# A two-layer trunk's attention layer, reordered by hand: 64 query-block steps, and the output projection interleaved with the last head

## Chip, cores and metric

The kernel runs on one core of one Trainium2 chip. The metric is the device time of one execution in microseconds (us). The engines are named as the profile names them: PE (matmul), PEld (weight load), DVE (VectorE), ACT (ScalarE), POOL (GpSimd) and SP, whose queue issues every DMA of this kernel.

## What is computed

The trunk has two layers on x of 1024 tokens by 1024 channels, each `x <- x + Mixer(RMSNorm(x))`, and a final RMSNorm. Layer 0 is a gated short convolution. Layer 1 is causal differential attention with 8 heads of two 64-wide maps each. Cut to what matters here:

```python
proj = h @ w_in                                    # h = rmsnorm(x); 1024 -> 4 * 1024
q, k, v, z = jnp.split(proj, 4, axis=-1)
logits = q_blk . k * 64**-0.5 + bias; causal       # 16 maps, query blocks of 128
p = softmax(logits)
a = p[map 0] - lam * p[map 1]                      # one pair of maps per head
o = rmsnorm(a @ v) * subln_g * (1 - lambda_init)   # per head, 128 wide
x = x + (o * silu(z)) @ w_out
return rmsnorm(x, final_g)
```

## The kernel before

All tensors lie transposed, channels on the partitions. Each weight and activation is split into a rounded part and a remainder ("h" and "l"), so one product is three matmuls per 128-channel slice (`mm3`, L132). A weight unit is a 128x1024 tile: a load (`wr`), an ACT copy that rounds it (`wh`, L119) and a POOL subtraction (`wl`, L120).

**Layer 0** (up to L380) is the same in both kernels but for the ring that its `x2` tiles use. Its last matmuls are the output projection `big<-yh,...`. Then `input_norm` sums the squares (`cps`, L157), takes the power -1/2 on POOL and spreads the row factors into `r_bc`.

**Layer 1** has for each head h: key, query and gate projections (`proj_qk`, `proj_z`: one unit, two halves of 512 tokens, 24 matmuls of 512 columns each), a value projection per pair of heads (`proj_v`, 256 columns a matmul), and 8 query blocks. A block's `scores` are matmuls into a PSUM tile `sc` (L514), a bias addition and a negated maximum on DVE (L517, L519), an exponential on ACT (L521), the combination of both maps on DVE (L528), a split into two f16 parts (ACT L533/L534/L537, POOL L535 or DVE L538), and a DMA that transposes them (L540). `values` multiplies the transposed parts of two blocks with v (L554, tile `av`). `head_norm` squares half a head's output on ACT (L565), splits it into three bf16 parts on POOL (L147, L148), sums columns on PE, takes the power on POOL (L571), writes 512 factors to DRAM (`rrd`), reads them back spread over all partitions (`rb`) and multiplies them in on POOL (L580). `proj_z` then multiplies by the gate on POOL (L407) and stores to `yd`.

The second layer's keys and low parts, `kt` and `qt`, each pass through a DMA that moves 64 partitions (`lo`, L432/L433; `qt`, L439/L440).

**What sets the order.** Python emits heads one after another; `attention(h)` is emitted at a raised priority (`AHEAD = 4000`), and a list scheduler of the language layer, which estimates times, chooses each engine's order from all emitted instructions. Each engine then runs its own queue strictly in that order. `behind` keeps two pairs of blocks between scores and values:

```python
for i, g in enumerate(order(h)):
    for qi in range(2):
        scores(h, g, qi)
        if qi == 0 and len(behind) == 2:
            with tc.issue_after(heads[h]["last", 2 * g].ins):
                attend(*behind.pop(0))
    behind.append((h, i, g))
```

Buffers that matter: PSUM has 3 `mm` tiles, 2 `sc` tiles and 1 `av` tile; `wh`/`wl` have two buffers each, so the unit after next waits for a unit's last matmul.

**The end.** `out_part` computes the output projection for tokens 0 to 511 (8 units of 24 matmuls of 512 columns), then 512 to 767 and 768 to 1023 (16 times 24 matmuls of 256 columns); `finish` applies the final norm and stores.

Of the kernel before, what the change touches and what calls it, by code (L numbers as in the profile page):

```python
# [11 lines left out]
F32 = mybir.dt.float32  # L12
# [10 lines left out]
P = 128  # L23
D = 1024
# [26 lines left out]
def trunk(ctx: ExitStack, tc: tile.TileContext, a: dict, out: bass.AP):  # L51
# [139 lines left out]
    def norm_rows(rsrc, dst, n, tags):  # L191

        for b0 in range(0, n, 4):
            nb = min(4, n - b0)
            dgs = sl.tile([P, 2, nb, P], F32R, tag=tags[b0 // 4 % len(tags)], name="dg")
            dgs = dgs[:, 0], dgs[:, 1]
            spread(rsrc[:, b0:b0 + nb], dgs, V)
            bps = rows(dgs, nb, (psm, "mm") if b0 else None)
# [159 lines left out]
    xh, xl = new_x()  # L358
    acc = sl.tile([P, S], F32, tag=t_acc, name="acc")
    for d in range(KC):  # L360
# [5 lines left out]
        x2 = r_t.tile([P, S], F32, name="x2")  # L366
# [12 lines left out]
    def input_norm():  # L379
        norm_cols([acc, sq], KC, rcol, (r_xr.tile([P, S], F32, name="r1"), r_xr.tile([P, S], BF16, name="r2")))  # L380
        norm_rows(rcol, r_bc, KC, [t_acc, t_xr[0]])


    r_wr.tags.append("wr1")
    heads = [dict() for _ in range(NH)]

    def proj(src, halves=(0, 1)):

        wh, wl = unit(src)
        for half in halves:  # L390
            s = HALF[half]
            pt = psm.tile([P, 512], F32, tag="mm", name="mm")
            mm3(pt, wh, wl, xh, xl, ((0, s.start, 512),))
            yield half, s, pt

    def proj_z(h, keep=None):

        for half, s, pt in proj(a["w_in1"][2 * NH + h]):
            with tc.high_priority():
                zr = sm.tile([P, 512], F32, tag="tq", name="zr")  # L400
                V.tensor_tensor(out=zr, in0=pt, in1=r_bc[:, s], op=ALU.mult)
            th = sm.tile([P, 512], F32, tag="hi", bufs=2, name="th") if keep is None else keep[:, s]
            A.activation(out=th, in_=zr, func=AF.Tanh, scale=0.5)
            V.scalar_tensor_tensor(out=th, in0=th, scalar=1.0, in1=zr, op0=ALU.add, op1=ALU.mult)
            if keep is None:
                o = heads[h]["o"]
                G.tensor_tensor(out=o[:, s], in0=o[:, s], in1=th, op=ALU.mult)  # L407
                dma(out=yd[h, half], in_=o[:, s])

    def proj_qk(h, kind, norm=None):  # L410


        own = (slice(0, HD), slice(HD, P))
        heads[h][kind] = tiles = {}
        if kind == "k":
            for m in range(2):
                tiles[m] = r_k.tile([P, S], F32R, name="kt")
        for half, s, pt in proj(a["w_in1"][(NH if kind == "k" else 0) + h], dict.fromkeys(g // 2 for g in order(h))):
            if norm and half == 0:
                norm()  # L420
            if kind == "q":
                for m in range(2):
                    tiles[m, half] = r_q.tile([P, 2, 512], F32R, name="qt")
            with tc.high_priority():
                tq = sm.tile([P, 512], F32, tag="tq", name="tq")
                if kind == "k":
                    V.scalar_tensor_tensor(out=tq, in0=pt, scalar=HD ** -0.5, in1=r_bc[:, s],
                                           op0=ALU.mult, op1=ALU.mult)
                    lo = sm.tile([P, 512], F32R, tag="lo", bufs=2, name="lo")
                    for m in range(2):  # L430
                        A.activation(out=tiles[m][own[m], s], in_=tq[own[m]], func=AF.Copy)
                        (G, V)[m].tensor_tensor(out=lo[own[m]], in0=tq[own[m]], in1=f(tiles[m])[own[m], s], op=ALU.subtract)  # L432
                        dma(out=f(tiles[m])[own[1 - m], s], in_=f(lo)[own[m]])  # L433
                else:
                    V.tensor_tensor(out=tq, in0=pt, in1=r_bc[:, s], op=ALU.mult)
                    for m in range(2):
                        qt = tiles[m, half]
                        A.activation(out=qt[own[m], 0, :], in_=tq[own[m]], func=AF.Copy)
                        G.tensor_tensor(out=qt[own[m], 1, :], in0=tq[own[m]], in1=f(qt)[own[m], 0, :], op=ALU.subtract)  # L439
                        dma(out=f(qt)[own[1 - m], ::-1, :], in_=f(qt)[own[m]])  # L440

    def proj_v(j, halves=range(4)):


        ws = [unit(a["w_v"][j, i]) for i in range(2)]
        if 0 in halves:
            vh, vl = (r_v.tile([P, KC, 256], F16, name="vt") for part in range(2))
            aux = sm.tile([P, 2, 256], F32, tag="dgl", name="aux")
            sq = sm.tile([P, 256], F32R, tag="sqw", name="sq")
            for k in range(KC):  # L450
                A.activation(out=aux[:, min(k, 1), :], in_=f(ws[k // 4][0])[:, (k % 4) * 256:(k % 4 + 1) * 256],
                             func=AF.Square, scale=g_sb[:, 1, k:k + 1])
                if k:
                    V.tensor_tensor(out=sq if k == KC - 1 else aux[:, 0, :], in0=aux[:, 0, :], in1=aux[:, 1, :], op=ALU.add)
            nps = psa.tile([P, 512], F32, tag="av", name="nps")
            T.matmul(nps[:, :256], lhsT=ones_r, rhs=sq, start=True, stop=True)
            srow = sm.tile([P, 256], F32, tag="srow", name="srow")
            half = aux[:, 1, :].bitcast(I32)
# [3 lines left out]
            sd = aux[:, 0, :].rearrange("p (a b) -> p a b", b=P)  # L462
            G.tensor_tensor(out=sd, in0=srow.rearrange("p (a b) -> p a b", b=P),
                            in1=ident.unsqueeze(1).to_broadcast([P, 2, P]), op=ALU.mult)
            us = sm.tile([P, 2], F32, tag="us", bufs=2, name="us")
            V.reduce_sum(out=us, in_=sd, axis=AX)
            V.reciprocal(out=us, in_=us)
            for h in (2 * j, 2 * j + 1):
                heads[h]["v"] = vh, vl, us[:, h % 2:h % 2 + 1], srow
        vh, vl, _, srow = heads[2 * j]["v"]  # L470
        for tp in halves:
            pt = psm.tile([P, 2, 256], F32, tag="mm", name="mm")
            for i in range(2):
                ts = slice((2 * tp + i) * P, (2 * tp + i + 1) * P)
                for k in range(KC):
                    wh, wl = ws[k // 4]
                    kk = slice((k % 4) * 256, (k % 4 + 1) * 256)
                    T.matmul(pt[:, i, :], lhsT=xh[k][:, ts], rhs=wh[:, kk], start=(k == 0), stop=False)  # L478
                    T.matmul(pt[:, i, :], lhsT=xh[k][:, ts], rhs=wl[:, kk], start=False, stop=False)  # L479
# [292 lines left out]
```

## Time and profile before

| | us |
|---|---|
| median of 3 runs | 1168.45 (1165.59 to 1169.64) |
| the profiled execution's own time | 1168.5 |
| its span, first to last instruction | 1166.7 |
| PE, PEld busy | 1060.6 (91%), 893.4 (77%) |
| DVE, ACT, POOL busy | 605.6 (52%), 425.4 (36%), 573.3 (49%) |
| mean granted TensorE clock | 0.952 of 2.4 GHz |

The span and the execution's time differ by 1.8 us, which lie around the first and last instruction. PE's busy time overlaps between neighbouring matmuls, whose ends are modelled; a busy PE may still run at half clock, which the granted clock tells. "Idle" of an engine that has nothing due costs nothing: what counts is which wait ends last.

### The profile page before, as it was taken

Reading aid. Unit: us, or ns where it says so; the run is one execution under the profiler, and the core shown is the slowest. Engines: PE = TensorE matmul, PEld = TensorE weight load, DVE = VectorE, ACT = ScalarE, POOL = GpSimd, SP = SyncE. Lnnn points to the kernel's source line nnn. Section 1 sums busy time; section 2 is a strip of 40 time slices with the busy share of each in tenths; the row PEclk is TensorE's granted clock in tenths of the full one; section 3 lists DMA queues with packets and bytes.
Section 4 is the critical chain, followed back from the end, with each engine's and each line's share of the span. In section 5 each row is a group of like instructions: output and inputs, shape, how many; then the busy total and the mean of one; then the engine's idle time right before and its main releaser. Section 6 shows DMA issues by size and latency. Waiting matters only on the chain.

```text
span 1166.7 us, 15388 instructions
## 1 busy us (share of the span) xinstructions
PE 1060.6 (91%) x5960; PEld 893.4 (77%) x5960; DVE 605.6 (52%) x945; ACT 425.4 (36%) x705; POOL 573.3 (49%) x355
## 2 busy tenths in 40 slices
PE   8899999999999997999887979979899788984996
PEld 6678888888888885897776869768697677863896
DVE  5573323313314323397676757768588574874123
ACT  3221111111111322366543555536456344463232
POOL 7544334334334442438545575455756556353353
PEclk9899999999999998899899889999899899996998
DMA  5221111111112433335564583644934546475132
GB/s 181 76 71 55 40 51 54 45 47 54 52 40 78 149 123 107 86 71 108 136 101 104 100 143 102 103 110 94 149 88 96 138 82 143 107 177 130 55 113 96
DMA packets 124826, 112.41 MB, mean 96 GB/s; under 512 B 89249, under 2 KB 97105, under 8 KB 124753
## 3 DMA queue, kind: packets, MB, share of 16 engines
q1 hardware_dynamic: 124752, 111.42, 39.4%
q8 instruction: 47, 0.77, 0.3%
q14 instruction: 27, 0.21, 0.1%
HBM read 67.82 MB, written 12.12 MB: 69 GB/s over the span
## 4 chain that ended last, share of the span: by engine, by line
PE 60%; DMA 12%; POOL 10%; issue 8%; DVE 5%; ACT 3%; SPq 1%; POOLq 0%; DVEq 0%; ACTq 0%
PE big L132 35%; PE mm L132 14%; PE sc L514 4%; DMA qt<-qt 3%; DMA rrd<-rr 3%; POOL wl L120 3%; PE av L554 2%; PE mm L479 2%; DMA wr<-in_w_out 2%; PE mm L480 2%; PE mm L478 2%; POOL qt L439 1%; DMA rb<-rrd 1%; DMA p<-p 1%; POOL p L535 1%
## 5 line engine op out<-in xcount | busy, mean ns | idle before, releaser
L120 POOL TENSOR_TENSOR wl<-wr,wh 128x1024 fp32r<-128x1024 f32 x75 | 184.9, 2468 | 257.4 <-ACT wh L119 252.8
L119 ACT ACTIVATE wh<-wr 128x1024 fp32r<-128x1024 f32 x75 | 79.2, 1057 | 314.6 <-PE big L132 293.5
L132 PE MATMUL mm<-xh,wh 128*128 128x512 f32 (+1 forms) x432 | 170.3, 395 | 5.6 <-ACT xh L643 2.5
L132 PE MATMUL mm<-xl,wh 128*128 128x512 f32 (+1 forms) x432 | 170.2, 394 | 4.9 <-POOL xl L644 3.4
L132 PE MATMUL mm<-xh,wl 128*128 128x512 f32 (+1 forms) x432 | 168.8, 394 | 0.9 <-POOL wl L120 0.9
L132 PE MATMUL big<-xh,wh 128*128 128x512 f32 x464 | 143.8, 391 | 2.2 <-DVE cr L289 2.2
L132 PE MATMUL big<-xh,wl 128*128 128x512 f32 x464 | 143.6, 390 | 0.0
L132 PE MATMUL big<-xl,wh 128*128 128x512 f32 x464 | 143.6, 391 | 0.0
L521 ACT ACTIVATE p<-sc,nm 128x256 f32<-128x256 f32 (+7 forms) x128 | 93.8, 736 | 96.4 <-DVE nm L519 55.5
L514 PE MATMUL sc<-kt,qt 128*128 128x512 f32 (+2 forms) x384 | 93.1, 366 | 23.3 <-DMA qt<-qt 21.5
L132 PEld LDWEIGHTS big<-xh,wh 128*128 128x128 f32 x464 | 87.3, 188 | 20.6 <-issue 2.6
L132 PEld LDWEIGHTS big<-xh,wl 128*128 128x128 f32 x464 | 87.6, 189 | 18.2
L132 PEld LDWEIGHTS big<-xl,wh 128*128 128x128 f32 x464 | 87.5, 189 | 18.1
L132 PEld LDWEIGHTS mm<-xl,wh 128*128 128x128 f32 x432 | 83.7, 194 | 21.6 <-POOL xl L644 4.1
L132 PEld LDWEIGHTS mm<-xh,wh 128*128 128x128 f32 x432 | 83.6, 194 | 21.0 <-ACT xh L643 3.1
L132 PEld LDWEIGHTS mm<-xh,wl 128*128 128x128 f32 x432 | 83.8, 194 | 16.5 <-POOL wl L120 1.4
L514 PEld LDWEIGHTS sc<-kt,qt 128*128 128x128 f32 x384 | 68.7, 200 | 34.4 <-issue 23.3
L519 DVE TENSOR_REDUCE nm<-sc 128x2 f32<-128x256 f32 (+5 forms) x96 | 90.9, 950 | 1.3
L554 PE MATMUL av<-p,vt 128*128 128x128 f16 x864 | 59.2, 229 | 24.8 <-DMA p<-p 24.3
L580 POOL TENSOR_TENSOR o<-o,rb 128x512 f32<-128x512 f32 x16 | 20.6, 1286 | 123.5 <-DMA rb<-rrd 114.9
L554 PEld LDWEIGHTS <-vt 128*128 128x128 f16 x864 | 53.0, 103 | 30.5 <-issue 18.2
L479 PE MATMUL mm<-wl,xh 128*128 128x256 f32 x256 | 74.8, 293 | 1.5 <-POOL wl L120 1.5
(174 smaller groups left out, 2026.2 us busy)
## 6 DMA issues: line engine op xcount, KB each, us to landing
wr<-in_w_in SPq DMA_DIRECT2D x53, 512.0 KB, 3.6
wr<-in_w_out SPq DMA_DIRECT2D x16, 512.0 KB, 4.4
qt<-qt SPq DMA_DIRECT2D x32, 256.0 KB, 5.1
xr<-in_xT SPq DMA_DIRECT2D x15, 512.0 KB, 4.4
wr<-in_w_v SPq DMA_DIRECT2D x14, 512.0 KB, 3.7
x2d<-x SPq DMA_DIRECT2D x8, 512.0 KB, 2.9
kt<-lo SPq DMA_DIRECT2D x32, 128.0 KB, 2.7
rb<-rrd SPq DMA_DIRECT2D x16, 256.0 KB, 4.9
```

Source lines behind the costliest of these rows:

```text
L119: A.activation(out=wh, in_=wr, func=AF.Copy)
L120: G.tensor_tensor(out=wl, in0=wr, in1=f(wh), op=ALU.subtract)
L132: T.matmul(ps[:, o:o + n], lhsT=w[:, s], rhs=r[k][:, t:t + n], start=(k == 0 and r is rh and w is wh), stop=(k == KC - 1 and w is wl))
L439: G.tensor_tensor(out=qt[own[m], 1, :], in0=tq[own[m]], in1=f(qt)[own[m], 0, :], op=ALU.subtract)
L478: T.matmul(pt[:, i, :], lhsT=xh[k][:, ts], rhs=wh[:, kk], start=(k == 0), stop=False)
L479: T.matmul(pt[:, i, :], lhsT=xh[k][:, ts], rhs=wl[:, kk], start=False, stop=False)
L480: T.matmul(pt[:, i, :], lhsT=xl[k][:, ts], rhs=wh[:, kk], start=False, stop=(k == KC - 1))
L514: hd["last", qb] = T.matmul(sc[:, i, c0:c1_], lhsT=qt[:, var, ts], rhs=kt[:, c0:c1_], start=(var == 0), stop=(var == 1))
L519: V.tensor_reduce(out=nm[:, ms], in_=sc[:, :, :L], axis=AX, op=ALU.max, negate=True)
L521: A.activation(out=(p1_, p2_)[m][:, :L], in_=sc[:, i, :L], func=AF.Exp, bias=nm[:, m:m + 1], accum_out=st[:, m:m + 1])
L554: T.matmul(av[:, qi * P:(qi + 1) * P], lhsT=v[:, kb, es], rhs=at[:, r, :], start=(kb == 0 and r == 0 and v is vh), stop=(kb == qb and v is ...
L580: G.tensor_tensor(out=o, in0=o, in1=rb, op=ALU.mult)
```

## The change

Layer 1 is put under a manual schedule: every engine runs in the order in which Python emits. The emission is a pipeline of 64 steps, one per query block of each head, step s = 8h + block. A table (`plan`) gives most steps one half projection of a later or earlier head, and the step function writes down the order:

```diff
+    for h in range(1, NH):
+        s0 = 8 * h + 2
+        if h < L7:
+            add_v((h + 1) // 2, (h + 1) % 2, (s0, s0 + 1))
+            add("k", h + 1, (s0 + 2, s0 + 4))
+            add("q", h + 1, (s0 + 3, s0 + 5))
+            add("z", h - 1, (s0 + 6, s0 + 7))
+        else:
+            add("z", L7, (s0, s0 + 1))
+            add("z", h - 1, (s0 + 2, s0 + 3))
...
+    def step(s, score=True):
+        h, qb = divmod(s, 8)
+        for u in loads.get(s, ()):
+            u.load()
+        todo, evict[:] = evict[:], []
+        for fn in todo:
+            fn()
...
+        if last:
+            last.first()
...
+        if score:
+            scores(h, qb)
+        if bounds:
+            half.sums(int(half is last))
+        for u in preps.get(s, ()) if s else ():
+            u.prep()
+        if isinstance(last, Values) and last is not half:
+            last.second()
+        if half and s:
+            half.mm()
+        if last and not isinstance(last, Values):
+            last.second()
+        if 0 <= s - 1 < NS - 1:
+            differences(*divmod(s - 1, 8))
+        if last:
+            last.third()
+        store_factors()
...
+        if s % 2 == 0 and 0 <= s - 4 < NS:
+            values(ph, pqb // 2)
+        if sqo and s < NS - 1:
+            head_sums(*sqo)
...
+        for what in fetches.get(s, ()):
+            fetch_factors(*what)
```

`last` is the half projection of step s-1, whose evictions (`first`, `second`, `third`) follow a step later; `prep` is a unit's `wh` and `wl`, made in the step before its first matmul at the latest; `differences` is the second part of the old `scores`. The head norm loses its bf16 split, and its factor is multiplied in beside the gate, from an `rb` that was fetched a step or two earlier:

```diff
+        def multiply(self):
+            o = heads[self.h]["o"][:, self.s]
+            for factor in (rbs.pop((self.h, self.half)), self.th):
+                G.tensor_tensor(out=o, in0=o, in1=factor, op=ALU.mult)
+            if self.h < L7 - 1:
+                dma(out=yd[self.h, self.half], in_=o)
...
+        cps = col_sums([sq], 4)
```

At the start, three half projections stand ahead of the sums of squares, one more between the sums and the row factors:

```diff
+        for s in (-4, -3, -2):
+            plan[s].mm()
+        def between():
+            for u in preps[-1]:
+                u.prep()
+            plan[-1].mm((pss, "sc"))
+
+        input_norm(between)
```

At the end, parts of the output projection run on the heads that are done (the last argument names the heads summed):

```diff
+        elif s == 63:
+            splits(2, 0)
+            differences(L7, 7)
+            for d in (0, 2, 3):
+                pts[d] = psm.tile([P, 512], F32, tag="mm", name="mm")
+                part(pts[d], d, 0, 512, (0, 1))
...
+    def tail():
+        for d in (0, 2, 3):
+            part(pts[d], d, 0, 512, (2, 3))
+        head_sums(*last_squares)
+        gate_last(0)
+        step(NS, False)
+        rest = last_factors(0, r_p1.tags[4])
+        splits(4, 0)
+        split_y(L7 - 1, 0, heads[L7 - 1]["o"][:, HALF[0]])
+        prep_w(1)
...
+        for d in (0, 2, 3):
+            part(pts[d], d, 0, 512, (4, 5, 6))
+        pts[1] = pss.tile([P, 512], F32, tag="sc", name="big")
+        part(pts[1], 1, 0, 512, range(7))
+        step(NS + 1, False)
+        rest(psa.tile([P, 512], F32, tag="av", name="bps"))
...
+        part(pts[4], 4, 0, 512, range(7))
+        step(NS + 2, False)
+        step(NS + 3, False)
...
+        for d in (0, 2, 3, 1, 4):
+            part(pts[d], d, 0, 512, (7,))
+            out_take(d, pts[d], 0, 512, x3a, accs)
```

The remainders of the fetched heads (`split_y`) and of the output weights (`prep_w`, with one more ACT pass for the gain) are all made on DVE. `finish` is a generator whose POOL multiplications are emitted between those of the next part.

How instructions moved, first on POOL around a head in the middle. In the rows, `o<-o,rb` is the head norm's factor, `o<-o,th` the gate, `wl` a weight unit, `qt` a query half's remainder. Before:

```order
L580 TENSOR_TENSOR o<-o,rb 128x512
L535 TENSOR_TENSOR p_4836<-p_4835,p_4836 128x768
L432 TENSOR_TENSOR lo<-tq,kt 64x512
L147 TENSOR_TENSOR r_4919<-sqo 128x512
L148 TENSOR_TENSOR r_4920<-r_4919 128x512
L120 TENSOR_TENSOR wl<-wr,wh 128x1024
```

In the changed kernel:

```order
L408 TENSOR_TENSOR wl<-wr,wh 128x1024
L640 TENSOR_TENSOR p_6406<-p_6405,p_6406 128x1024
L494 TENSOR_TENSOR o<-o,rb 128x512
L494 TENSOR_TENSOR o<-o,th 128x512
L408 TENSOR_TENSOR wl<-wr,wh 128x1024
L494 TENSOR_TENSOR o<-o,rb 128x512
```

The factor's multiplication now stands right before its gate's, and the two `r` passes are gone.

Second, PE at the end of layer 0. Before, the sums `cps` come right after the last `big` rows:

```order
L132 MATMUL big<-yl_458,wh 128x512 x2
L132 MATMUL big<-yh_450,wl 128x512 x2
L157 LDWEIGHTS acc
L157 MATMUL cps<-ones_85,acc 128x1
L157 LDWEIGHTS r_2887
L157 MATMUL cps<-ones_85,r_2887 128x1
L132 MATMUL mm<-xh_2320,wh 128x512
```

In the changed kernel 72 `mm` matmuls, three half projections, follow the same `big` rows:

```order
L132 MATMUL big<-yl_458,wh 128x512 x2
L132 MATMUL big<-yh_450,wl 128x512 x2
L132 MATMUL mm<-xh_2320,wh 128x512
L132 MATMUL mm<-xl_2328,wh 128x512
L132 MATMUL mm<-xh_2320,wl 128x512
L132 MATMUL mm<-xh_2321,wh 128x512
```

The sums moved behind the projections' matmuls, which don't need them.

Third, PE at the end of layer 1, in the changed kernel (`xh`, `xl` are here the output projection's moving tiles, `wo` its weights). The rows before the last pair of blocks are matmuls on heads 0 to 6:

```order
L132 MATMUL big<-xh_8371,wo 128x512
L132 MATMUL big<-xh_8372,wo 128x512
L132 MATMUL big<-xl_8380,wo 128x512
L132 MATMUL big<-xh_8372,wo 128x512
L659 LDWEIGHTS vt
L659 MATMUL av<-p_8393,vt 128x128
```

Before, head 7's last two blocks stood 13 such matmuls apart, with its sums right behind; now 69 such matmuls stand between its third and its last pair of blocks.

## Rows read from the trace of the kernel before

**Rows 1.** Busy time by stretch: us, PE, PEld, DVE, ACT, POOL, clock, DMA, GB/s

```profile
457.00:500.00 43.00, 33.96 (x179) 28.30 (x179) 20.19 (x29) 15.91 (x24) 19.18 (x11) 0.84 0.34 98
500.00:1010.00 510.00, 454.34 (x3026) 391.72 (x3025) 359.36 (x646) 261.74 (x484) 294.79 (x185) 0.95 0.54 109
1010.00:1080.00 70.00, 48.60 (x266) 37.63 (x265) 43.12 (x55) 33.76 (x48) 28.26 (x20) 0.83 0.63 145
457.00:1156.00 699.00, 611.15 (x3993) 526.66 (x3992) 440.32 (x767) 335.98 (x602) 377.78 (x245) 0.93 0.51 110
```

**Rows 2.** Waits in layer 1: us in total, times, longest

```profile
POOL o L580 <- DMA rb<-rrd: 114.9, 14, 13.6
PE av L554 <- DMA p<-p: 24.3, 4, 11.1
```

**Rows 3.** Chain of waits, 600 to 621 us: start, us, what

```profile
600.60 11.95 issue
...
618.96 2.37 POOL wl L120
```

**Rows 4.** Busy time by stretch (columns as in Rows 1), around that wait

```profile
605.00:610.00 5.00, 1.54 (x26) 1.37 (x26) 0.48 (x1) 0.43 (x3) 0.00 (x0) 1.00 0.64 92
610.00:615.00 5.00, 5.00 (x26) 4.21 (x24) 3.62 (x9) 3.29 (x9) 2.42 (x2) 0.66 0.48 100
```

**Rows 5.** Busy time by stretch, layer 0 without waits

```profile
100.00:150.00 50.00, 50.00 (x222) 41.41 (x221) 14.04 (x15) 6.54 (x7) 21.94 (x14) 1.00 0.17 53
```

**Rows 6.** Chain of waits: dense pieces of PE at full clock

```profile
991.07 2.53 PE av L554 x45
...
1122.16 18.35 PE mm L132 x153
```

**Rows 7.** PE's timeline: layer 0's end and the first scores

```profile
456.53 0.61 PE L132 MATMUL big<-yh,wl 128*128 128x512 f32 x2
...
465.82 0.79 PE L132 MATMUL mm<-xh,wh 128*128 128x512 f32 x1 [2.28 <-ACT wh L119]
...
495.75 0.71 PE L514 MATMUL sc<-kt,qt 128*128 128x256 f32 x4
```

**Rows 8.** Instruction groups of layer 1: busy us, mean ns, idle before

```profile
L517 DVE TENSOR_TENSOR sc<-sc,bias 128x256 f32<-128x256 f32 x72 | 30.3, 424 | 31.2 <-PE sc L514 29.9 <-PE cps L157 1.3
L519 DVE TENSOR_REDUCE nm<-sc 128x1 f32<-128x1024 f32 x16 | 19.5, 1218 | 0.3
L528 DVE SCALAR_TENSOR_TENSOR p<-p,cs,p 128x1024 f32<-128x1024 f32 x8 | 15.5, 1939 | 0.0
L427 DVE SCALAR_TENSOR_TENSOR tq<-mm,r_bc 128x512 f32<-128x512 f32 x16 | 10.9, 684 | 10.4 <-ACT r_bc L200 5.9 <-POOL lo L432 2.4 <-PE mm L132 2.0
L644 DVE TENSOR_TENSOR xl<-yr,xh 128x512 fp32r<-128x512 f32 x6 | 7.8, 1313 | 0.9 <-ACT xh L643 0.9
L119 ACT ACTIVATE wh<-wr 128x1024 fp32r<-128x1024 f32 x38 | 40.0, 1054 | 20.1 <-PE mm L480 10.5 <-DMA wr<-in_w_in 4.2 <-issue 2.6
L521 ACT ACTIVATE p<-sc,nm 128x1024 f32<-128x1024 f32 x16 | 17.7, 1108 | 6.9 <-issue 4.0 <-DVE nm L519 1.9 <-PE mm L132 1.0
L120 POOL TENSOR_TENSOR wl<-wr,wh 128x1024 fp32r<-128x1024 f32 x38 | 94.8, 2500 | 41.6 <-ACT wh L119 36.9 <-DVE sc L517 3.1 <-ACT p L521 1.4
L535 POOL TENSOR_TENSOR p<-p,p 128x1024 f16<-128x1024 f32 x8 | 17.4, 2170 | 19.2 <-ACT p L534 19.0
```

**Rows 9.** DMA issues: median us from issue to landing

```profile
rb<-rrd SPq DMA_DIRECT2D x16, 256.0 KB, 4.9
p<-p SPq DMA_TRANSPOSE x64, 3.8
```

**Rows 10.** Timeline of DVE: one combination, no instruction on POOL beside it

```profile
1044.97 1.28 DVE L528 SCALAR_TENSOR_TENSOR p<-p,cs,p 128x1024 f32<-128x1024 f32 x1
```

**Rows 11.** PE's timeline: the wait for the last transposed block

```profile
1063.75 2.74 PE L554 MATMUL av<-p,vt 128*128 128x128 f16 x24 [11.05 <-DMA p<-p]
```

**Rows 12.** Timeline of DVE: the eviction behind the last projection matmul

```profile
1156.09 0.42 DVE L669 TENSOR_TENSOR x<-mm,xr 128x256 f32<-128x256 f32 x1 [2.45 <-PE mm L132]
```

More of the change, by code (lines that the diff above doesn't have):

```diff
@@ L378, in trunk, with input_norm @@
                 G.tensor_tensor(out=acc, in0=acc, in1=sq, op=ALU.add)
-    def input_norm():
+    def input_norm(between):
         norm_cols([acc, sq], KC, rcol, (r_xr.tile([P, S], F32, name="r1"), r_xr.tile([P, S], BF16, name="r2")))
-        norm_rows(rcol, r_bc, KC, [t_acc, t_xr[0]])
-    r_wr.tags.append("wr1")
[L385 to L394, printed above, removed]
@@ L442, in proj_v @@
[L442 to L451, printed above, removed]
-                             func=AF.Square, scale=g_sb[:, 1, k:k + 1])
-                if k:
-                    V.tensor_tensor(out=sq if k == KC - 1 else aux[:, 0, :], in0=aux[:, 0, :], in1=aux[:, 1, :], op=ALU.add)
+        between()
@@ L597, in attention @@
         dma(out=bias, in_=bass.AP(src.tensor, src.offset, [[1, P], [STRIP, 2], [1, 256]]))
-        for i, g in enumerate(order(h)):
-            for qi in range(2):
-                scores(h, g, qi)
-                if qi == 0 and len(behind) == 2:
-                    with tc.issue_after(heads[h]["last", 2 * g].ins):
-                        attend(*behind.pop(0))
-            behind.append((h, i, g))
-    AHEAD = 4000
-    def order(h):
-        return (3, 2, 1, 0) if h in DESC else (0, 1, 2, 3)
@@ L634, in trunk, with unit_of, add @@
-    next(norms.pop())
-    sz7 = r_k.tile([P, S], F32, name="sz7")
-    proj_z(L7, sz7)
-    o7 = heads[L7]["o"]
-    yh, yl = new_x()
-    r_yr = Ring(sl, [r_k.tags[1], r_q.tags[r_q.n % 5]])
+    plan, units = {}, []
+    def unit_of(src, step):
+        units.append([step, step, Unit(src)])
+        return units[-1]
+    def add(kind, h, steps):
+        cls, base = {"k": (Key, NH), "q": (Query, 0), "z": (Gate, 2 * NH)}[kind]
+        u = unit_of(a["w_in1"][base + h], steps[0])
+        u[1] = steps[1]
+        for half, step in enumerate(steps):
+            plan[step] = cls(u[2], half, h)
@@ new lines, in trunk @@
+    units.sort(key=lambda x: x[0])
+    loads, preps, when = {}, {}, {}
+    for i, (_, _, u) in enumerate(units):
+        when[i] = max(units[i - 2][1] + 1, when[i - 1], -1) if i > 1 else -9
+        preps.setdefault(when[i], []).append(u)
+        loads.setdefault(max(when[i - 2] + 1, -1) if i > 1 else -9, []).append(u)
+    fetches = {}
+    for t, half in plan.items():
+        if isinstance(half, Gate) and half.h < L7:
+            fetches.setdefault(t - 1 + half.half, []).append((half.h, half.half))
@@ new lines, in prelude @@
+    def prelude():
+        for u in loads[-9]:
+            u.load()
+        units[0][2].prep()
+        units[1][2].prep()
+        for u in loads[-1]:
+            u.load()
+        for s in (-4, -3, -2):
[5 more added lines that the diff above has]
+        input_norm(between)
+        plan[-4].first()
+        plan[-4].second()
+        plan[-2].first()
+        plan[-3].first()
+        plan[-3].second()
+        bias_of(0)
+        for u in preps[0]:
+            u.prep()
+        plan[0].mm()
```

537 lines of the change are left out of this document (364 added, 173 removed).

## The prediction, written before the changed kernel ran

> **What bounds the kernel now.** Begin with the stretches. Layer 0 runs 222 matmuls of 512 columns in 50.00 us at the full clock of 2.4 GHz, 0.225 us each, with no gap [rows 5]: nothing is to be won there. Layer 1 is another matter. From 457 to 1156 us PE is busy for 611.15 of 699.0 us at a mean granted clock of 0.93, while DVE (440), POOL (378) and ACT (336) are far from full [rows 1]. So PE sets the time, and it loses some of it twice: 88 us idle, and part of the busy time at 1.2 GHz.
>
> How much is lost follows from the work. Prices at full clock: 0.225 us for 512 columns [rows 5]; 18.35 / 153 = 0.12 us for 256 columns and 2.53 / 45 = 0.056 us for a matmul of the values [rows 6]. Counted from the changed kernel's order, layer 1 has 1152 + 192 + 10 matmuls of 512 columns (projections, first half of the output, row factors): 304.7 us. It has 768 + 384 of 256 columns (v, second half of the output): 138.2 us. The scores are 151,552 columns, at 0.225 us per 512 that is 66.6 us. The values are 864, 48.4 us; small sums add some 4 us. Together **562 us** in 699: 137 us are lost, 88 as idle time and 49 at the low clock, about 0.55 us of slow work for each us of idle.
>
> Next, who keeps PE waiting. Waits of PE itself name few culprits (24.3 us for transposed blocks, 11.05 of it once in the last head [rows 2, 11]); one step further back stands POOL, which waited 114.9 us in 14 pieces for `rb` [rows 2]. The chain shows how this reaches PE: 11.95 us without work, then the weight unit `wl` only at 618.96 us [rows 3]. While POOL stands, PE is busy for 1.54 of 5 us, and in the next 5 us the granted clock is 0.66, partly the 1.2 GHz level [rows 4]. POOL's queue is in order: one instruction whose factor is still on its way holds the weight units and query remainders behind it.
>
> **The parts of the change.**
>
> *Factor beside the gate.* The 14 multiplications by `rb` move behind the gate's projection, and `rb` is asked for one to two steps (7 to 14 us) before, against a landing of 4.9 us [rows 9]. POOL's 114.9 us of waiting go. The two bf16 passes per half head go too; I cost that at nothing, since POOL is not late otherwise. Behind such a wait now stand only `wl` units that have a step of slack. This is the main gain, and it can return no more than the 137 us.
>
> *Start of layer 1.* Before, PE stops from 457.1 us to 465.82 us, and the first scores start at 495.75 us [rows 7]. Now 72 matmuls (16.2 us) cover the squares' sums, but the row factors come only behind them: the power, its spreading and 24 more matmuls end near 481 us, then the key and query halves must be evicted, split and moved by DMA. By hand this chain puts the first scores at 495 us again (481 + 0.7 us eviction + copies + two POOL passes of about 1.4 us after the keys' + about 5 us of DMA). Bounds: 489 if the evictions overlap better, 500 if the queries queue longer. I take 495.75, unchanged. By then the changed kernel has done 96 matmuls of 512 and 48 of 256 columns, 27.4 us of work, so 562 - 27.4 = **534.6 us** remain.
>
> *The 61 full steps.* Per head the projections, scores and values cost PE about 60 us, 7 to 8 us a step. DVE's share before was 359.36 us for some 62 steps, 5.8 a step; ACT 4.2, POOL 4.8 [rows 1]: all below PE. Their order matters where one step is heavy. Take the last block of a head. Its scores take PE 1.8 us (8 x 0.225). DVE first does two evictions (1.2 us together), then for each of two maps 0.42 + 1.22 us: the second maximum is there at 4.5 us. The exponential takes 1.1 us and 0.2 to read its sum, the next unit's `wh` 1.05 and `wl` 2.5 [rows 8]: ready at 9.35 us. PE needs it at about 7.7 (step) + 0.5 (next scores) + 0.45 (two matmuls) = 8.7 us: 0.7 us late. In every second head DVE enters this step some 1.7 us behind, because the steps of blocks 4 and 5 ask of it about 9 us each against PE's 7. Mean 1.5, with hops between engines 2 us a head: 14 us for seven heads. Steps 8 and 9 have no projection; the value units' `wl` come about 7.5 us in, PE has 3.6 us of work until then: 4 us. The first four steps, where squares delay the exponentials: 4 us. Sum **22 us**; bounds 0 and, at 1 us for each of 61 steps, 61.
>
> The table puts one transposing DMA in each step; a block lands 3.8 us after issue [rows 9] and is used about two steps later, so I cost the queue at nothing. SP's queue is in order too: a load that waits for its buffer delays the step's transposition, and with that cover gone `values` would wait. Where `r_x2` and the residuals' buffers differ, nothing hangs on it.
>
> *The last steps and the output projection.* Steps 62 and 63 have no projection, and the splits of fetched heads stand in DVE's and ACT's queues behind scores and combination. From step 62: the first remainder is ready at 9.4 us, PE has finished scores and values at 6.1, so 3.3 us idle; the third head's remainder comes after the next combination, at 20.6 against 14.8: 5.8 us and 0.6 more; the remainders of heads 4 to 6 (1.31 us each [rows 8]) wait for head 7's row factors, whose power stands on POOL behind the last f16 subtraction (2.17 us [rows 8]): 33.2 against 27.4, 5.8 us and 1.9 more; 1.5 us go to `sc` buffers. Together **19 us**. What it removes is the wait of 11.05 us [rows 11]: the last block lands near 34 us, and PE has work on heads 0 to 6 until about 50. Bounds: 5 if the splits slip between other work, 35 if each wait grows by half and the second half's splits are late too.
>
> *Clock.* Some 23 us of my idle time (steps 8 and 9, the last steps) comes in pieces of 3 us and more; at 0.55 us of slow work per us, the ratio above from [rows 1], that costs **12 us**; bounds 0 and 30.
>
> *End.* Behind the last projection matmul the final norm stands as before: from 1156.0 (eviction at 1156.09 [rows 12]) to the span's end at 1166.7, **10.7 us**. POOL's earlier accumulations no longer stand behind four multiplications; that work was hidden from the end by PE, so nothing.
>
> *Sum.* 495.75 + 534.6 + 22 + 19 + 12 + 10.7 = 1094 us of span; with the 1.8 us around it **1096 us**, against 1168.5 of the profiled execution, which stands at the median of the runs (1168.45).
>
> **The rivals.**
>
> *A. The steps run nearly free of waits.* For it: before, most of the lost time leads back to POOL's waits [rows 2, 3], and those go. Without the 22 and half of the 19 and 12 us: 1096 - 22 - 16 = about 1058 to 1075 us.
>
> *B. DVE becomes the bound.* A combination of 1024 columns takes 1.28 us with nothing on POOL beside it, but 1.94 us in the mean [rows 8, 10]: two engines that read SBUF together slow each other. POOL, no longer standing still, now works beside DVE in most steps. With 1.5 us more in the heavy steps (blocks 4, 5 and 7, and their key remainders), DVE asks some 60 us of a head, no slack is left to catch up, and PE waits 5 to 6 us a head: 1096 + 40 = 1136 us. Against it: DVE's means already hold these collisions. The Trainium skill's SBUF — State Buffer, section "Who interferes with whom", says that a DVE instruction with two SBUF inputs and a GpSimd instruction that reads SBUF exclude each other, and that the second one to start blocks fully. By that rule the change would pay for the freed POOL with DVE's time, which is this rival's 1136 us.
>
> *C. Slower: the written order holds PE in every step.* The place is the chain scores, maximum, exponential, `wh`, `wl` to the next step's projection, priced at 9.35 us for the longest blocks. A scheduler could put other matmuls there; a written order can't. The gain of 72 us over 61 steps is gone when each step is 1.2 us longer than I forecast; at 2 us each with slow work behind (0.55 x 122, half of it) the time is 1096 + 122 + 34 = about 1250 us. Against it: short blocks leave this chain several us of slack.
>
> *D. A queue for DMAs holds it.* Loads, copies of 64 partitions and a transposition per step share SP, and one late load delays a block. At 4 us a head: 1096 + 32 = about 1128 us.
>
> **How the numbers follow.** Forecast (1080 to 1115 us) 0.50, A 0.18, B 0.18, D 0.09, C 0.05. The order shows that the change does what it says, so that is no rival. A range from 1066 to 1134 us holds the forecast, about two thirds of A and half of B and D: about 0.8. A measurement of this kernel can tell 0.3% (3.5 us) from no change; only C reaches 1165 us, part of it beyond. Faster 0.95, same 0.01, slower 0.04.
>
> **What would show it.** Right: POOL's wait for `rb` near zero; layer 1's PE idle time 45 to 60 us instead of 88 and its clock above 0.95; first scores near 495 us; PE's largest waits in the last two steps and the first output parts, on remainders (`xl`) from DVE; the last pair of blocks without a wait. Wrong: PE waiting on `wl` in every step (C), DVE above 90% busy through the heads (B), SP or transposed blocks among the first releasers (D), or a first score beyond 500 us.

## The result, and the profile after

The changed kernel is slower, by about 1.5%: 1187.75 us in the median of 4 runs (1182.53 to 1192.76) against 1169.05 us of the kernel before beside it, a ratio of 1.0149 (95% interval 1.0114 to 1.0185). I had forecast 1096 us and given "slower" a chance of 0.04. The profiled execution is the slowest of the four (1192.76 us); its span is 1191.0 us.

The stretch from the first scores to the last projection matmul, by stretch (us, PE, PEld, DVE, ACT, POOL busy, clock, DMA share, GB/s), answers to [rows 1]:

```profile
490.86:1040.90 550.04, 491.60 (x3062) 423.14 (x3062) 363.78 (x664) 282.74 (x514) 262.35 (x162) 0.93 0.64 109
1040.90:1180.30 139.40, 118.41 (x700) 101.46 (x698) 51.42 (x89) 52.96 (x85) 44.54 (x35) 0.88 0.32 98
...
490.86:1180.28 689.42, 609.99 (x3760) 524.58 (x3760) 415.20 (x753) 335.70 (x598) 306.87 (x197) 0.92 0.57 107
```

The first scores start at 490.86 us, 5 us earlier than before [rows 7]. From there PE is idle for 689.42 - 609.99 = 79.4 us, and the clock is lower than before. The DMA share of 0.64 is new: 0.54 stood in [rows 1].

The waits of the whole execution (us in total, times, longest), beside [rows 2]:

```profile
POOL o L494 <- DMA rb<-rrd: 51.2, 6, 10.8
...
ACT p L619 <- DMA p<-p: 24.6, 9, 8.9
...
PE mm L132 <- POOL wl L408: 20.3, 9, 5.2
...
ACT wr L854 <- DMA wr<-in_w_out: 17.3, 2, 15.3
...
PE cps L157 <- ACT sqo L668: 12.0, 1, 12.0
```

POOL's wait for `rb` has halved but not gone. In the trace POOL comes to the multiplication about 7.5 us after the fetch of a head's first half was issued, but only 3 to 4 us after that of four of the seven second halves and once before it; five of its six waits fall on second halves. ACT's waits on DMAs, which the kernel before also had, have grown: for transposed blocks (an exponential needs the buffer that a block's transposition still reads) from 15.7 us in 3 waits to 24.6 in 9, and for the output weights from 13.4 us, the longest 7.5, to 17.3, the longest 15.3. The DMA issues (median us to landing), first of the changed kernel, then the row of the kernel before that matters:

```profile
qt<-qt SPq DMA_DIRECT2D x32, 256.0 KB, 7.5
kt<-lo SPq DMA_DIRECT2D x32, 128.0 KB, 9.5
...
p<-p SPq DMA_TRANSPOSE x64, 4.3
...
rrd<-rr SPq DMA_DIRECT2D x14, 2.0 KB, 10.0
```

```profile
rrd<-rr SPq DMA_DIRECT2D x16, 2.0 KB, 9.8
```

The store of a half head's factors moves 2 KB, and takes 10 us to land: it is written as 512 single elements. (The changed kernel's trace has the landing of 3 of its 14 stores; the trace of the kernel before, with 9.8 us, agrees.) I had that row before me and read [rows 9] around it. What it does to its neighbours is seen in the changed kernel at 710 us (SP's timeline: start, us, what), in the stretch behind the store (columns as above, DMA share and GB/s last), in the DMA table of the piece in which the load behind the store is issued, and then on POOL and PE:

```profile
710.44 0.58 SPq L688 DMA_DIRECT2D rrd<-rr  x1
711.07 0.49 SPq L403 DMA_DIRECT2D wr<-in_w_in  x1
711.66 1.18 SPq L645 DMA_TRANSPOSE p<-p  x1
...
713.52 0.42 SPq L692 DMA_DIRECT2D rb<-rrd  x1
```

```profile
712.00:722.00 10.00, 10.00 (x105) 9.78 (x105) 5.11 (x9) 3.58 (x10) 2.37 (x1) 1.00 0.99 52
```

```profile
wr<-in_w_in SPq DMA_DIRECT2D x1, 512.0 KB, 13.1
```

```profile
727.13 1.27 POOL L494 TENSOR_TENSOR o<-o,rb 128x512 f32<-128x512 f32 x1 [9.62 <-DMA rb<-rrd]
...
729.90 2.34 POOL L408 TENSOR_TENSOR wl<-wr,wh 128x1024 fp32r<-128x1024 f32 x1
```

```profile
732.30 0.79 PE L132 MATMUL mm<-xh,wl 128*128 128x512 f32 x1 [2.45 <-POOL wl L408]
```

```profile
730.00:740.00 10.00, 7.70 (x27) 6.01 (x28) 5.50 (x16) 3.87 (x7) 7.67 (x6) 0.66 0.53 152
```

In the ten us from 712 us on, behind the store, the 16 DMA engines are busy for 0.99 of the time and move 52 GB/s, against 0.54 and 109 over the heads of the kernel before [rows 1]. The weight load that follows the store by 0.6 us lands 13.1 us after its issue, where the median of such loads is 3.7. `rb`, further back in the same queue, is late too: POOL comes to its multiplication 4.0 us after the fetch was issued and stands for 9.62 us, `wl` comes behind that, and PE waits 2.45 us; from 730 to 740 us its mean granted clock is 0.66, partly the 1.2 GHz level. It goes like this behind nearly every store: all 26 transfers that were issued within 4 us behind one, and whose landing the trace has, landed 11.4 to 14.5 us after their issue. The worst place lies at 983 us (SP, then the load's landing, then ACT, then the stretch on PE):

```profile
982.87 0.58 SPq L688 DMA_DIRECT2D rrd<-rr  x1
983.54 0.45 SPq L845 DMA_DIRECT2D wr<-in_w_out  x1
```

```profile
wr<-in_w_out SPq DMA_DIRECT2D x1, 512.0 KB, 12.3
```

```profile
995.88 1.15 ACT L854 ACTIVATE wr<-wr,gsub 128x1024 f32<-128x1024 f32 x1 [15.33 <-DMA wr<-in_w_out]
```

```profile
1000.00:1010.00 10.00, 0.67 (x4) 0.68 (x4) 8.10 (x12) 4.43 (x9) 5.01 (x3) 0.50 0.07 15
```

The written order asks for the first output weights in step 56 and has ACT scale them at the end of step 57. A late load there stops ACT for 15.33 us with the next exponentials, a weight unit and the squares behind it, and PE works 0.67 us of ten.

### The profile page after: what moved, and what is told of

Read it like the earlier page. It is cut to its first block, busy times and chain, and to the rows that moved or that the text cites. A ratio compares the mean times of both kernels' runs of the same rounds, so it can differ in the third digit from the quotient of the medians.

```text
span 1191.0 us, 15198 instructions
## 1 busy us (share of the span) xinstructions
PE 1090.4 (92%) x5900; PEld 916.7 (77%) x5900; DVE 598.1 (50%) x951; ACT 437.1 (37%) x715; POOL 517.2 (43%) x315
## 4 chain that ended last, share of the span: by engine, by line
PE 59%; DVE 11%; POOL 8%; issue 7%; DMA 7%; ACT 6%; SPq 1%; POOLq 0%; DVEq 0%; ACTq 0%
PE big L132 35%; PE mm L132 18%; POOL wl L408 3%; PE sc L612 2%; DVE nm L617 2%; DMA wr<-in_w_in 2%; DMA p<-p 2%; PE av L659 2%; DMA wr<-in_w_out 2%; DVE p L633 1%; PE mm L525 1%; DMA qt<-qt 1%; POOL o L494 1%; POOL qt L465 1%; ACT wh L407 1%
## 5 line engine op out<-in xcount | busy, mean ns | idle before, releaser
L132 PE MATMUL big<-xh,wh 128*128 128x512 f32 x472 | 147.2, 391 | 2.2 <-DVE cr L289 2.2
L119 ACT ACTIVATE wh<-wr 128x1024 fp32r<-128x1024 f32 x37 | 39.2, 1061 | 294.4 <-PE big L132 293.6
L132 PE MATMUL big<-xh,wl 128*128 128x512 f32 x472 | 146.8, 391 | 0.0
L132 PE MATMUL big<-xl,wh 128*128 128x512 f32 x472 | 146.4, 390 | 0.0
L612 PEld LDWEIGHTS sc<-kt,qt 128*128 128x128 f32 x384 | 67.4, 201 | 27.7 <-ACT p L619 16.1
L643 DVE SCALAR_TENSOR_TENSOR p<-p,cs,p 128x128 f16<-128x128 f32 (+4 forms) x40 | 46.9, 1174 | 68.6 <-ACT p L642 68.1
L525 PE MATMUL mm<-wh,xh 128*128 128x256 f32 x256 | 75.5, 295 | 0.8 <-DVE tq L460 0.6
```

The costliest lines, as they stand in the source:

```text
L119: A.activation(out=wh, in_=wr, func=AF.Copy)
L132: T.matmul(ps[:, o:o + n], lhsT=w[:, s], rhs=r[k][:, t:t + n], start=(k == 0 and r is rh and w is wh), stop=(k == KC - 1 and w is wl))
L525: T.matmul(self.pts[tp][:, i, :], lhsT=x[k][:, ts], rhs=w[:, kk], start=(k == 0 and i == 0 and x is xh and w is wh), stop=(k == KC - 1 and ...
L612: T.matmul(sc[:, i, c0:c1_], lhsT=qt[:, var, ts], rhs=kt[:, c0:c1_], start=(var == 0), stop=(var == 1))
L643: V.scalar_tensor_tensor(out=al, in0=p1_[:, :L], scalar=cs[:, 0:1], in1=ah, op0=ALU.mult, op1=ALU.subtract)
```

## The experiments

Theory S: these stores hold the one DMA queue, and in a written order what is late behind them stops whole engines. Rival W: the written order itself costs the time. The kernel before ran beside each batch on the same chip (1177.6 to 1179.9 us there), and the ratios are to it.

**Stores left out.** `store_factors` issues nothing, and `fetch_factors` reads a row that is there anyway:

```diff
-    dma(out=rrd[h, half].rearrange("(b p) -> p b", p=P), in_=rr)
...
-    dma(out=rb, in_=rrd[h, half].unsqueeze(0).partition_broadcast(P))
+    dma(out=rb, in_=x2d[h, half, :512].unsqueeze(0).partition_broadcast(P))
```

> Leaves out the 14 stores of the head-norm factors (512 single elements each); the factor tile is fetched from a row of x2d instead, so heads 0 to 6 are multiplied by other numbers. Theory S (a store of 512 single elements holds the one DMA queue for some 10 us, and what is issued behind it lands 12 to 14 us after issue instead of 4 to 5; in a written order the late load or block then stops the engine that waits, and all behind it): POOL's wait for rb falls from 51 us to under 12, the stall of 15 us of ACT for the output weights near 990 us goes, steps of block 4 fall to 7 to 9 us, clock in the heads over 0.96, time 1105 to 1145 us against 1187.75. Rival W (the written chain scores, exponential, wh, wl and DVE's ping-pong with ACT cost the time, whatever the DMAs do): landings get shorter but the time stays within 12 us, 1175 to 1195.

Measured: 1150.57 us, ratio 0.9752 (0.9718 to 0.9785), just above the range that S gave and far below W's. POOL's wait for the fetched factor falls from 51.2 to 7.6 us and ACT's for the output weights from 17.3 to 6.9, as S said. This run also takes away the fetch's dependence on the store; the 16-byte stores below keep it. The two stretches:

```profile
490.62:999.00 508.38, 475.56 (x3062) 411.22 (x3062) 372.21 (x664) 280.30 (x513) 262.90 (x162) 0.97 0.53 117
999.00:1138.00 139.00, 116.67 (x700) 99.97 (x698) 51.50 (x89) 53.64 (x86) 44.54 (x35) 0.89 0.33 101
```

Against the changed kernel the stretch of the scores is 41.7 us shorter (550.04 to 508.38); the rest is as long as it was. So the stores cost some 42 us, all of it in the heads, and something else costs time in the rest.

**Stores from ACT's queue.** `nc.scalar.dma_start` for the same store.

> The same stores, issued from ACT's DMA queue instead of SP's; the output is complete. Theory S with the queue's order as the cost: within 15 us of the run without stores, 1110 to 1155 us, and the loads on SP land in 4 to 8 us also beside a store. Theory S with the DMA engines themselves as the cost (the single elements fill them whatever queue they come from): loads beside a store still land some 10 us late, 1165 to 1190 us. Rival W: 1180 to 1200 (ACT's issue of about 0.6 us per store added).

Measured: 1168.14 us, ratio 0.9902 (0.9873 to 0.9932): in the range of S's second case, in which the elements fill the DMA engines whatever queue they come from. The landings agree with that case. The store itself still takes 10 us; a load issued on SP 0.5 us after the store of 756.26 us lands after 15.2 us (second row); and PE now waits for blocks, which it did not in the changed kernel:

```profile
rrd<-rr ACTq DMA_DIRECT2D x14, 2.0 KB, 10.2
```

```profile
wr<-in_w_v SPq DMA_DIRECT2D x1, 512.0 KB, 15.2
```

```profile
PE av L659 <- DMA p<-p: 11.4, 4, 4.3
```

The Trainium skill's page DMA: Bandwidth & Descriptors, section "Queues, rings and completion order", says that both queues feed the same 16 DMA engines, which take packets from them in turn; the late landings on the other queue agree with it. So it is not only the place in SP's queue that costs. Still, against the changed kernel this gives back 0.0247 of the 0.0397 that leaving the stores out gave. POOL's wait for `rb` falls from 51.2 to 18.8 us with it; why the other late landings cost less here is not shown.

**The written order taken off.** `layer1()` without the written order.

> The written order is taken off: the same instructions, order left to the list scheduler, all of layer 1. Rival W (the written order is what costs): faster by over 30 us, 1110 to 1158 us, with fewer waits of PE in the heads. Theory S: the stores clog the queue in any order; the scheduler fills some of the gaps: 1150 to 1195 us, landings behind stores still 10 us and more.

Measured: 1135.01 us, ratio 0.9627 (0.9586 to 0.9667). That is inside W's range and below the one that S gave: the written order costs 0.05. That the stores cost time stands all the same, by the two runs above; they are still there, and POOL waits for `rb` more than ever:

```profile
POOL o L494 <- DMA rb<-rrd: 156.0, 14, 16.8
```

POOL stands three times as long as in the written order (51.2 us), and the time is shorter: how long an engine stands does not tell by itself what it costs.

**The tail in list order.** The written order ends with step 63.

> The written order ends with step 63; everything behind it (values of the last blocks, output projection, final norm) is left to the list scheduler. If the tail's written order is what makes it 160 us from step 62 to the end against my 129: 1155 to 1170 us, from fewer waits behind 1040 us. Theory S, in which the tail is long since head 7's last steps come late and slow: within 8 us of the changed kernel, 1180 to 1196, step 62 unchanged near 1030 us.

Measured: 1162.13 us, ratio 0.9855 (0.9801 to 0.9910); the stretch behind the scores shrinks from 139.4 to 106.8 us, at a clock of 0.96:

```profile
1045.50:1152.30 106.80, 103.62 (x700) 91.79 (x698) 52.88 (x89) 52.98 (x85) 44.29 (x35) 0.96 0.41 127
```

That is the range of the first case, so the tail's written order costs too. Both theories hold a part, so the second batch shortens the store and keeps its data.

**Stores of 16 bytes.** Row by partition, 128 elements of 16 bytes; the multiplication reads the factor with a stride of four words:

```diff
-    dma(out=rrd[h, half].rearrange("(b p) -> p b", p=P), in_=rr)
+    dma(out=rrd[h, half].rearrange("(p b) -> p b", b=4), in_=rr)
...
-    for factor in (rbs.pop((self.h, self.half)), self.th):
-        G.tensor_tensor(out=o, in0=o, in1=factor, op=ALU.mult)
+    o4 = o.rearrange("p (b q) -> p b q", b=4)
+    rb4 = rbs.pop((self.h, self.half)).rearrange("p (q b) -> p b q", b=4)
+    G.tensor_tensor(out=o4, in0=o4, in1=rb4, op=ALU.mult)
+    G.tensor_tensor(out=o, in0=o, in1=self.th, op=ALU.mult)
```

> The changed kernel with each store of head-norm factors as 128 elements of 16 bytes instead of 512 of 4 (row by partition; the multiplication reads the fetched factor with a stride of 4 words). The output is complete. If the number of elements is what holds the queue (512 hold it about 10 us, so 128 some 2.5): ratio to the kernel before 0.972 to 0.985, near the 0.975 of the run without stores. If a store into DRAM costs its time whatever its elements are: 1.00 to 1.02, as the changed kernel. A strided read that slows POOL much would show as multiplications well over their 1.2 us and take some of the gain back.

Measured: 1152.33 us, ratio 0.9774 (0.9744 to 0.9804): nearly all of what leaving the stores out gave. Every engine runs its instructions in the same order as in the changed kernel, and the multiplication with the stride takes 1.64 us in the mean instead of 1.39, which takes back little. The landings (to be compared with those of the changed kernel) and the two stretches:

```profile
qt<-qt SPq DMA_DIRECT2D x32, 256.0 KB, 3.7
kt<-lo SPq DMA_DIRECT2D x32, 128.0 KB, 3.9
...
rrd<-rr SPq DMA_DIRECT2D x14, 2.0 KB, 3.0
```

```profile
491.20:1001.42 510.22, 480.18 (x3061) 415.69 (x3062) 376.84 (x664) 280.49 (x514) 266.13 (x162) 0.95 0.54 118
1001.42:1143.29 141.87, 119.26 (x700) 102.53 (x698) 51.79 (x89) 53.13 (x85) 44.81 (x35) 0.86 0.32 96
```

A quarter of the elements takes 3.0 us instead of 10.0.

**16-byte stores and the tail in list order.**

> Both edits: 16-byte stores, and the written order ends with step 63. If store and tail are two separate costs they add: 0.975 - 0.029 = 0.946, between 0.940 and 0.955. If the tail only looked costly because head 7 came late behind the stores, the second edit adds under 1%: 0.965 to 0.980.

Measured: 1121.77 us, ratio 0.9519 (0.9495 to 0.9543). The two costs add, as nearly as the ranges tell. The profile then shows where the written steps still lose time (the last row is the tail, in list order):

```profile
490.95:605.00 114.05, 97.61 (x617) 85.53 (x618) 82.50 (x150) 58.91 (x118) 51.13 (x32) 0.93 0.46 103
605.00:965.00 360.00, 353.21 (x2329) 305.81 (x2327) 263.90 (x468) 203.42 (x367) 206.59 (x126) 0.99 0.60 126
965.00:1000.87 35.87, 25.85 (x120) 20.63 (x118) 28.21 (x48) 18.07 (x30) 8.43 (x6) 0.83 0.39 94
1000.87:1107.80 106.93, 103.51 (x700) 91.73 (x698) 53.97 (x89) 52.78 (x85) 44.90 (x35) 0.96 0.40 126
```

From 605 to 965 us, five heads and more, PE is idle for 6.8 us of 360 at a clock of 0.99: the written order runs freely there. Ahead of that it loses 16.4 us of 114, behind it 10 us of 36.

**16-byte stores, everything in list order.**

> 16-byte stores, all of layer 1 left to the list scheduler. In the run with the list order POOL still waited 156 us for rb behind the stores. If the stores cost there too: 0.925 to 0.950. If the scheduler had already covered them with other work: 0.955 to 0.968, as without this edit (0.963). Against the run with only the tail in list order it tells what the written order of the 64 steps is worth: lower than it, nothing.

Measured: 1082.00 us, ratio 0.9186 (0.9158 to 0.9213), the fastest kernel here, and faster than either case gave: in list order the short stores give 0.044, no less than in the written one.

```profile
488.70:1067.65 578.95, 558.83 (x3740) 490.62 (x3738) 435.14 (x753) 329.91 (x595) 317.43 (x196) 1.00 0.53 125
```

PE is idle for 20 us and the clock rounds to 1.00, so 559 us is about what this work takes at full clock.

**The kernel before with 16-byte stores**, the same edit and nothing else.

> The kernel before with 16-byte stores and nothing else. If the single-element stores were what lay behind POOL's 114.9 us of waiting for rb there: ratio 0.955 to 0.985, with that wait halved. If those waits came from the fetch being asked for too late (its 4.9 us of landing and the order): 0.995 to 1.005.

Measured: 1108.53 us, ratio 0.9406 (0.9381 to 0.9432), more than either case gave. The list scheduler's order hardly changes with the edit (POOL's is the same). POOL's wait for `rb` falls from the 114.9 us of [rows 2], and PE's own waits on DMAs, for query copies and for blocks, nearly go; first the kernel before (for blocks it had 24.3 us [rows 2]), then this run:

```profile
PE sc L514 <- DMA qt<-qt: 21.5, 6, 6.6
```

```profile
POOL o L581 <- DMA rb<-rrd: 65.1, 12, 7.4
...
PE sc L514 <- DMA qt<-qt: 5.3, 3, 3.0
PE av L554 <- DMA p<-p: 5.1, 2, 3.7
```

So the stores were a large loss of the kernel before as well: 69 us for the form of 16 small stores, half of the 137 us that the prediction counted as lost.

**The written order in the middle alone.** Steps 16 to 57 are written, all else is left to the scheduler.

> 16-byte stores; the written order holds for steps 16 to 57 alone, the start of layer 1, steps 0 to 15, steps 58 to 63 and the tail are left to the list scheduler. If what the written order still costs with short stores lies at its two ends (late weight units in the first heads, the output weights and squares of steps 58 to 63, the tail), the middle is free: ratio 0.915 to 0.928, as with the list order everywhere (0.919). If it costs in every step (the chain to wl, DVE and ACT in turn): 0.935 to 0.952.

Measured: 1090.14 us, ratio 0.9251 (0.9219 to 0.9282). Most of what the written order costs lies at its ends; the middle costs about 0.0065 against list order everywhere, with some 0.003 of uncertainty on either ratio.

**The multiplication right behind its fetch**, written order, 16-byte stores:

```diff
     dma(out=rb, in_=rrd[h, half].unsqueeze(0).partition_broadcast(P))
+    o4 = heads[h]["o"][:, HALF[half]].rearrange("p (b q) -> p b q", b=4)
+    G.tensor_tensor(out=o4, in0=o4, in1=rb.rearrange("p (q b) -> p b q", b=4), op=ALU.mult)
```

(and no longer in `multiply`).

> The written order throughout, 16-byte stores, but the multiplication by the fetched factor stands right behind its fetch and not beside the gate, so POOL waits there for a landing of some 4 us, 14 times. If the place of this multiplication is worth what I forecast (a standing POOL holds the weight units, and PE): 0.990 to 1.010, 15 to 35 us over the run with 16-byte stores alone (0.977). If only landings of 10 us and more did harm: 0.975 to 0.985.

Measured: 1219.50 us, ratio 1.0363 (1.0337 to 1.0389), worse than either case: 0.059, some 69 us, over the same kernel with the multiplication beside the gate.

```profile
POOL o L693 <- DMA rb<-rrd: 98.2, 12, 10.4
...
PE mm L524 <- POOL wl L408: 55.3, 12, 8.6
```

In these 12 waits POOL comes to the multiplication 1.4 to 4.6 us before the fetch is even issued, and the landing takes 4 to 6 us more, some 8 us each time. POOL stands 98.2 us, and PE waits 55.3 us for the weight units behind it.

**The changed kernel again**, beside these.

> The changed kernel once more, beside the others on one chip: 1.010 to 1.020 if ratios carry over between chips; if not, every ratio above has to be read within its own batch.

Measured: 1192.08 us, ratio 1.0124 (1.0097 to 1.0151). The ratios carry over between chips.

**Written to step 57.** The start is written as well, steps 58 to 63 and the tail are not.

> 16-byte stores; written order from the start of layer 1 to step 57, the rest (steps 58 to 63 and the tail) in list order. Beside 0.925 (written in steps 16 to 57 alone) and 0.952 (written to step 63) it divides the 0.027 between them. From the profile of the latter: 17 us idle and some 6 us of slow work between 491 and 605 us against 6 us idle with the list order, so the start costs 15 to 18 us: 0.937 to 0.942, and steps 58 to 63 the other 12 to 17 us. If the last steps cost all of it: 0.922 to 0.930; if the start does: 0.947 to 0.955.

Measured: 1106.04 us, ratio 0.9391 (0.9358 to 0.9425). The start up to step 15 costs 0.014, steps 58 to 63 cost 0.013.

Put in a row, each line taking one cost out of the changed kernel:

| kernel | ratio to before | step, us of 1178 |
|---|---|---|
| changed | 1.0124 to 1.0149 | |
| 16-byte stores | 0.9774 | 41 to 44 |
| and the tail in list order | 0.9519 | 30 |
| and steps 58 to 63 | 0.9391 | 15 |
| and the start up to step 15 | 0.9251 | 16.5 |
| and steps 16 to 57 | 0.9186 | 8 |
| before, with 16-byte stores | 0.9406 | |

With the stores as they were, the new arrangement of the work is worth 0.037 if a scheduler orders it (0.9627), and the written order then costs 0.05. That is how the change comes out slower. With short stores the written order costs 0.059 (0.9774 against 0.9186), and the arrangement is worth 0.022 (0.9406 against 0.9186).

## Why the prediction was wrong

Against the forecast's span of 1094 us, with work and idle time counted from the first scores to the last projection matmul:

| term | forecast | changed kernel |
|---|---|---|
| first scores | 495.75 | 490.86 |
| work at full clock | 534.6 | 558.8 (all in list order, 16-byte stores) |
| PE idle | 22 + 19 | 79.4 |
| slow clock | 12 | 609.99 - 558.8 = 51.2 |
| end | 10.7 | 10.7 |

*The step that failed* is the sentence "so I cost the queue at nothing". It rested on the medians of [rows 9], 3.8 and 4.9 us, and on a use "one to two steps" later. A median over 64 transfers hides 14 stores, behind which what is issued next lands 11 to 15 us after its issue. The forecast left the store's own row out, and asked how long each transfer takes but not what is queued in front of it; for half the fetches of `rb` the lead was 4 us and not 7 to 14. Shortening the store alone gives 41 to 44 us back. Rival D named the place, "one late load delays a block", but priced it without the store, at 4 us a head and 1128 us; its signs are the ones that came.

The queue is the largest single term, but not the whole miss of 92 us: with short stores the changed kernel still takes 1152.33 us, above the range. Of the 60 us by which that profiled span, 1154.1 us, exceeds 1094, the work was forecast 24 us too short and the idle time 12 us (52.7 against 41), and the slow clock took 41 us in place of 12; the first scores came 5 us earlier.

*What bounds the kernel now* was wrong for the kernel before. The prediction found few culprits among PE's own waits and went one step back to POOL. It passed over the row of 21.5 us for query copies; with the 24.3 us for blocks, 45.8 us of PE's idle time ended at a DMA, some 21 us of it at one issued within 9 us behind a store, and only 2.4 us at a weight unit. The idle time of [rows 4], by which it showed how POOL reaches PE, ended at a transposed block that was issued 3 us behind a store (PE's timeline, then SP's):

```profile
609.52 1.47 PE L554 MATMUL av<-p,vt 128*128 128x128 f16 x18 [3.46 <-DMA p<-p]
```

```profile
597.62 0.38 SPq L574 DMA_DIRECT2D rrd<-rr  x1
...
600.63 5.12 SPq L540 DMA_TRANSPOSE p<-p  x2
```

POOL stood at the same time, for an `rb` out of the same queue. With short stores the 45.8 us became 10.4, the 114.9 us of [rows 2] became 65.1, and the time fell by 6% with the order nearly unchanged. The mechanism itself exists in the written order: the run with the multiplication behind its fetch shows 98.2 us on POOL, 55.3 us on PE and 69 us in time. The change moved the instruction that waited; what made everything late stayed, and the next users in the queue (weight loads, blocks, key and query copies) waited instead.

*Start of layer 1*: within its bounds of 489 to 500. The 72 matmuls cover the sums of squares: PE is busy for 30.48 of the 33.86 us from 457 us to the first scores.

*The 61 full steps*: the 14 us for a late `wl` behind each head's last block did not come. With short stores the five middle heads lose 6.8 us of 360, 0.7 us of it for `wl`. What I put at 4 + 4 us, the first steps and steps 8 and 9, lost 16.4 us of 114 in that profile.

*The last steps and the output projection*: with short stores the tail's idle time is 141.87 - 119.26 = 22.6 us and that of the steps ahead of it 10 us, inside my bounds of 5 to 35 though over the 19 that I took. But in list order, with the same stores, the same tail has 3.4 us of idle time (106.93 - 103.51) and is busy for 103.51 instead of 119.26 us, at a clock of 0.96 instead of 0.86. So nearly half of what the written tail costs is slow work, 15.8 us, for which the forecast had about 10 (0.55 x 19).

*Clock*: the ratio of 0.55 us of slow work for each us of idle time was, if anything, low: 51.2 / 79.4 = 0.64, and 0.77 with short stores. Wrong was to apply it only to 23 us of long waits.

*Work*: 24 us too little. PE is busy 16.1 us with the column sums of the squares, where I had put all small sums at 4. Taken from each matmul's start to the next one's in the fastest run, the column sums take about 14 us, the scores 74 where I had counted 66.6, and the matmuls of 512 columns 289 where I had 283; that is the whole of it.

```profile
L157 PE MATMUL cps<-ones_r,sqo 128*128 128x1 f32 x128 | 16.1, 247 | 12.0 <-ACT sqo L668 12.0
```

*Rivals*: A, a pipeline nearly free of waits, is what the middle became once the store was short. B fell: DVE is busy for 66% of the heads (363.78 of 550.04 us), and its combination of 1024 columns got shorter, 1.62 us in the mean against 1.94 [rows 8]. C gave the right sign for the wrong reason: the chain to `wl` did not hold the steps. Of the signs for "right", the last pair of blocks without a wait came; `rb` near zero, idle time of 45 to 60 us and a clock above 0.95 did not.

## What to carry to other kernels

Before a written order is costed, list for each queue what stands in it, and behind every transfer of many small elements add its own landing time to that of all that follow, on the other queue too; a median to landing does not show this. Follow an engine's idle time to the instruction that ended it before blaming another engine that stood at the same time. When many things wait for DMAs, look first for the one transfer that makes them late and make that one short, and only then move what waits. The written order never paid here: in the steady middle, where every step is alike, it cost about 8 us, and at the start, the last steps and the tail some 60 more than the list order. A kernel may use both, and a run with each tells which part is worth writing.

## What the runs showed of the hardware

The landing of a 2 KB store went with the number of its elements: 512 of 4 bytes 10.0 us, 128 of 16 bytes 3.0 us, about 18 ns for each element more, an estimate from these two. The Trainium skill's page DMA: Bandwidth & Descriptors, section Specifications, gives 512 bytes as the least for the full rate; the elements here have 4 and 16. What was issued within 4 us behind the longer store landed after 11 to 15 us instead of about 4, and in part also when the store went out from another queue.

DVE's combination of 128 columns took 1.23 us in the mean in the changed kernel, against 0.63 us before:

```profile
L633 DVE SCALAR_TENSOR_TENSOR p<-p,cs,p 128x128 f32<-128x128 f32 x8 | 9.8, 1228 | 0.0
```

```profile
L528 DVE SCALAR_TENSOR_TENSOR p<-p,cs,p 128x128 f32<-128x128 f32 x8 | 5.0, 628 | 0.0
```

The same instruction took twice as long by its place in the order alone. In the timelines of the kernel before, the three that had no POOL instruction beside them took 0.35 us, and the mean is made by one of 2.59 us beside a weight unit. In the changed kernel all eight had one beside them, two a weight unit and the others mostly an f16 subtraction or a factor's multiplication, and took 0.91 to 2.14 us. So POOL's work beside it goes with the longer time; not every POOL instruction lengthens it, and no run here takes one away to show it.
